# Feed-forward output projections by seven half-size products (Strassen) in a two-layer hybrid trunk

## The chip, the cores and the metric

The kernel runs on one core of one Trainium2 chip. The metric is device time in microseconds (us), median of several runs; lower is better. TensorE (PE) multiplies matrices, with its weight loads listed apart as PEld; VectorE (DVE), ScalarE (ACT) and GpSimd (POOL) do elementwise work; SyncE (SP) issues most DMAs. Each engine works through its own queue of instructions in order.

## What is computed

A decoder trunk of two layers on x, 512 tokens by 1024 features, in float32. Each layer has a token mixer (gated linear attention, GLA, in the first; gated DeltaNet, GDN, in the second) and then a gated convolutional feed-forward layer. After each of these four sublayers stands a layer norm of a scaled residual:

```python
D_MODEL, SEQ, D_FF, ALPHA = 1024, 512, 2816, 4 ** 0.25

def conv_ffn(x, w_in, conv_w, w_out):            # w_in 1024 x 5632, w_out 2816 x 1024
    h = causal_dwconv(x @ w_in, conv_w)          # 3 taps along the tokens, per channel
    gate, up = jnp.split(h, 2, axis=-1)
    return (jax.nn.gelu(gate, approximate=False) * up) @ w_out

for i in range(2):
    y = gla_mixer(h, ...) if i == 0 else gdn_mixer(h, ...)
    h = layer_norm(ALPHA * h + y, ln_g[i, 0], ln_b[i, 0])
    h = layer_norm(ALPHA * h + conv_ffn(h, ...), ln_g[i, 1], ln_b[i, 1])
```

## The kernel before, in words

The code numbers the sublayers 0 (GLA), 1 (feed-forward), 2 (GDN) and 3 (feed-forward); "layer 1" and "layer 3" below are the two feed-forward ones.

**Precision.** Every projection multiplies two float32 operands, each split into a rounded part and its residue (`split_out`, L450: ScalarE casts `wh`, VectorE subtracts for `wl`, both on L451). A product is three matmuls: high by high, high by low, low by high (`tm_terms`, L362; all matmuls are issued in `mm`, L161).

**Layout.** x lies transposed in SBUF as `xh` and `xl` (feature blocks by tokens). An up-projection item (`fm_items`, L339) makes one block of 128 hidden features by 512 tokens in a PSUM bank `fm`: 8 input blocks times 3 terms, 24 matmuls of 128x512. While the layer norm before it is not done, the first four items (`HEADSTART`) are done in two halves of 256 tokens, so that they can start with the first two token blocks. For each of the 22 feature blocks there is a gate item and an up item. `ffn` (L719) runs three taps on each (`ffn_conv`: ScalarE L714, VectorE L716 twice), a Gelu on the gate (L726), their product (L731), and splits the result into `gh` and `gl`.

**Output projection before.** The 22 feature blocks are taken in two chunks (`CHUNKS`: 12 and 10). After the items of a chunk, `out_proj` (L403) multiplies by the rows of w_out: for each half of the 1024 output columns, four PSUM banks `tm` (one per block of 128 tokens, `tb`) accumulate over the pairs of feature blocks (`tm_half`, L367). When a bank is done, VectorE adds it to the residual `h` (L412 the first time with ALPHA, then L414). In the last chunk it also takes statistics (L419) and starts the layer norm of that token block; there the last four pairs of the second half (`TAIL`) are done token block by token block, with their weights held in slots, so that the layer norms start one after another.

**Layer norm.** `ln_stats` (L588) aggregates the statistics; `ln` (L606) normalizes h, transposes it on TensorE (`xT`), applies gain and bias on ScalarE (`xf`) and writes `xh` and `xl`; after the last sublayer `ln_out` (L652) does the final norm on VectorE and stores.

**Weights.** `plan` lists the weight tiles in order of use. `issue` (L221) loads one of 128x1024 from HBM into `raw` (3 buffers, `RAWB`) on SP's queue and splits it into `wh` and `wl` (4 buffers each, `WB`); `prefetch` does so `LOOKAHEAD` (2) tiles ahead in the order of the program. That order is a priority: the queue of each engine is filled at build time, with what is ready first. `self.clk` and `self.dve` are the program's own estimates of TensorE's and VectorE's time; generators (`spawn`, `pump`) emit side work, such as layer norms, when that clock has reached their due time.

**Memory.** One SBUF pool of 53 slots of 128x512 (`slot`) serves all sublayers, the residual and the split activations too; constants have their own pool (`keep`). PSUM has 8 banks (`psum`).

Of the kernel before, what the change touches and what calls it, by code (L numbers as in the profile page):

```python
# [25 lines left out]
ALPHA = 4.0 ** 0.25  # L26
LN_EPS = 1e-5
# [3 lines left out]
CHUNKS = ((0, 12), (12, 22))  # L31
SLOTS = 53
# [16 lines left out]
def blk(i, n=P):  # L49
    return slice(i * n, i * n + n)  # L50


class Trunk:
# [3 lines left out]
    def __init__(self, ctx, tc):  # L57
        self.tc = tc
        self.nc = nc = tc.nc
        self.n = 0  # L60
        ec = ctx.enter_context
        ap = ec(tc.tile_pool(name="acts", bufs=1))
        self.xh = ap.tile([P, NC, S], F32R, name="xh", tag="xh")
        self.xl = ap.tile([P, NC, S], F32R, name="xl", tag="xl")
        self.wp = ec(tc.tile_pool(name="wts", bufs=WB))
        self.mp = ec(tc.tile_pool(name="mem", bufs=SLOTS))
# [4 lines left out]
        self.dp = ec(tc.tile_pool(name="scratch", bufs=1, space=bass.MemoryType.DRAM))  # L71
        self.ident = self.keep([P, P], "ident")
# [5 lines left out]
        self.reset = self.keep([P, S], "reset")  # L78
        nc.vector.memset(self.reset, 1.0)
        nc.vector.memset(c4(self.reset)[:, :, 0:1], 0.0)  # L80
        self.h = None
        self.plan = []
        self.issued = 0
        self.taken = 0
# [12 lines left out]
        self.late = []  # L97
        self.first = None
        self.between = None
# [5 lines left out]

    def slot(self, s, dt=F32):
        return self.mp.tile([P, S], dt, name=self.uid(s), tag="slot")
# [4 lines left out]
    def small(self, shape, s, dt=F32, bufs=None):  # L112
        return self.sp.tile(shape, dt, name=self.uid(s), tag=s, bufs=bufs)

# [41 lines left out]
    def mm(self, out, a, b, start=True, stop=True):  # L156
# [4 lines left out]
        t = self.nc.tensor.matmul(out, a, b, start=start, stop=stop)  # L161
# [54 lines left out]

    @staticmethod
    def in_slots(item):
        return item[0] == "tm" and item[5]

    def issue(self, item):  # L221

        nc = self.nc
        if item[0] == "rep":
            return self.issue_rep(*item[1:])
        raw = self.rp.tile([P, 1024], F32, name=self.uid("raw"), tag="raw")
# [57 lines left out]

    def prefetch(self):
        while self.issued < min(len(self.plan), self.taken + self.look):
            item = self.plan[self.issued]
            if self.held == WB and not self.in_slots(item):
                break
            self.ready.append(self.issue(item))  # L290
            self.issued += 1

# [46 lines left out]
    def fm_items(self, items):  # L339

        start = 0 if all(self.is_set(("x", tb)) for tb in range(NTB)) else HEADSTART
        first = items[:start]
        ws, banks = [], []
        for half in range(2 if first else 0):
            self.wait(("x", 2 * half), ("x", 2 * half + 1))
            for i, f in enumerate(first):
                if not half:
                    ws.append(self.weight())
                    banks.append(self.psum("fm"))
                self.fm_mms(banks[i], ws[i], half * 256, half * 256 + 256, self.pin and not half and i < 2)  # L350
                if half:
# [10 lines left out]
    def tm_terms(self, ps, ah, al, wh, wl, first, last):  # L362
        self.mm(ps, ah, wh, first, False)
        self.mm(ps, ah, wl, False, False)
        self.mm(ps, al, wh, False, last)
# [137 lines left out]
    def load_x(self, x):  # L503

        nc = self.nc
        self.h = [[self.slot("h") for _ in range(2)] for _ in range(NTB)]
# [99 lines left out]
    def ln(self, tb, spill=False):  # L606
# [36 lines left out]
        yield from self.until(("x", NTB - 1))  # L643
# [8 lines left out]
    def ln_out(self, tb, out):  # L652
        nc = self.nc
        gb, h = self.ln_gb(), self.h[tb]

        def center(mv):
            for hf in range(2):
                nc.vector.scalar_tensor_tensor(h[hf], h[hf], mv[:, 0:1], gb[hf], ALU.subtract, ALU.mult)

        mv, rs = self.ln_stats(tb, center)  # L660
        for hf in range(2):
            m = 2 if tb == NTB - 1 and hf else 1
            for i in range(m):
                cols = blk(i, S // m)
                nc.vector.scalar_tensor_tensor(h[hf][:, cols], h[hf][:, cols], rs, gb[2 + hf][:, cols],
                                               ALU.mult, ALU.add)
                (nc.sync, nc.scalar)[i].dma_start(out[blk(tb), hf * S + cols.start:hf * S + cols.stop],
                                                  h[hf][:, cols])
        yield 0.0

    def unspill(self, gb_rows):
# [4 lines left out]
        for hf in range(2):  # L676
            for tb in range(NTB):
                t = self.slot("h")
# [17 lines left out]
    def ffn_plan(self, w_in, w_out):  # L696
        for f0, f1 in CHUNKS:
# [3 lines left out]
            self.plan_out(w_out, f0 * P, f1 - f0, TAIL if f1 == NF else 0)  # L701
# [8 lines left out]
    def ffn_conv(self, ps, cw, b):  # L710
        nc = self.nc
        a = self.slot("conv")
# [6 lines left out]
    def ffn(self, cw, li, g, b, final, out=False):  # L719
        nc = self.nc  # L720
        for ci, (f0, f1) in enumerate(CHUNKS):
            gs, act, items = [], {}, []
            for f in range(f0, f1):
                def gate(ps, f=f):
                    a = self.ffn_conv(ps, cw, f)
# [3 lines left out]
                def up(ps, f=f):  # L729
                    u = self.ffn_conv(ps, cw, NF + f)  # L730
                    nc.vector.tensor_mul(u, u, act.pop(f))  # L731
                    t = self.slot("gh", F32R), self.slot("gl", F32R)
                    self.split_out(*t, u)
                    gs.append(t)
# [3 lines left out]
            last = ci == len(CHUNKS) - 1  # L738
# [5 lines left out]
            a = lambda c, tb: (gs[c][0][:, blk(tb)], gs[c][1][:, blk(tb)])  # L744
            self.out_proj(a, f1 - f0, ci == 0, final if last else None, 2 if last and out else 1)
# [38 lines left out]
    def gla_consts(self, w_gk2, b_gk, norm_w):  # L784
        nc = self.nc

        self.gk2 = self.keep([96, S], "gk2", F32R)
# [13 lines left out]
        self.gla_nw = self.keep([P, 256], "gla_nw")  # L801
# [8 lines left out]
        self.gla_mask = self.keep([P, S], "gla_mask", U8)  # L810
        nc.gpsimd.tensor_copy(self.gla_mask, mk)
        self.b_gk = self.keep([P, 4], "gla_b")
        self.spawn(self.columns([(b_gk.rearrange("(n p) -> n p", p=P), 4, self.b_gk)]), 12.0)

    def gla(self, li, g, b):
# [83 lines left out]
        ss = self.keep([P, GH, 4], "gla_ss")  # L899
        rr = self.keep([P, GH, 4], "gla_rr")  # L900
# [89 lines left out]
    def mixer_out(self, y, li, g, b, final=None):  # L990
# [7 lines left out]
        self.out_proj(a, NC, True, self.ln)  # L998

# [24 lines left out]
    def gdn_conv(self, ps, b):  # L1024

        nc = self.nc
        a = self.slot("conv")
# [8 lines left out]
    def gdn(self, li, g, b):  # L1036
        nc = self.nc
        self.flags = {f: t for f, t in self.flags.items() if f[0] in ("x", "h")}
        hs = slice(H0, H0 + 8)
        al = self.gdn_al  # L1040
        spilled = self.gb_rows
        keep = lambda s: self.keep([P, DH, 4], s)
        eb, neb, ebl, cd = (keep(s) for s in ("gd_eb", "gd_neb", "gd_ebl", "gd_cd"))
        bn, bp, rk = keep("gd_bn"), keep("gd_bp"), keep("gd_rk")
        ssq, rr = self.keep([P, 2, DH, 4], "gd_ssq"), self.keep([P, DH, 4], "gd_rr")
        bt = self.keep([P, 4, 64], "gd_bt")
# [7 lines left out]
        def ba_done(ps):  # L1054
# [8 lines left out]
            ea = self.keep([P, 1], "gd_ea")  # L1063
# [50 lines left out]
        def k_done(ps, hd):  # L1114
            k[hd] = self.gdn_conv(ps, 8 + hd)
# [4 lines left out]
        def q_done(ps, hd):  # L1120
            q[hd] = self.gdn_conv(ps, hd)
# [134 lines left out]
        def v_done(ps, hd):  # L1256
            vc[hd % 2] = self.gdn_conv(ps, 16 + hd)
# [145 lines left out]
def kernel(  # L1403
# [41 lines left out]
    t.drain()  # L1445

# [28 lines left out]
```

## Time and profile before

| | |
|---|---|
| median of 3 runs | 1276.69 us (1276.61 to 1277.08) |
| profiled execution: first to last instruction | 1274.8 us (the page gives no other time for it; the median lies 1.9 above) |
| matmuls | 6682 |
| busy: PE, VectorE, ScalarE, GpSimd | 1260.9, 785.5, 552.2, 112.5 us |
| DMA | 126.53 MB, mean 99 GB/s |
| mean granted TensorE clock | 0.999 |

How to read it: the page is one execution. "Busy" counts the instructions of an engine; matmuls overlap in the array, so the sum of their durations is more than the time that they take. A row of a group or of the timeline gives start, duration, engine, line, operation, output and inputs, shape, and in brackets the idle time before it and who ended that. A row of waits gives who waited for whom, total us, times, longest. A row of the chain gives start, us, and what. A row of a stretch gives its bounds and length, then busy time (and number) of PE, PEld, VectorE, ScalarE, GpSimd, then granted clock, DMA share and GB/s.

### The profile page before, as it was taken

How to read it: one execution, taken by the hardware profiler on the slowest of the kernel's cores; microseconds unless marked ns; L12 is line 12 of the kernel's file. 1: busy time of each engine (PE TensorE's matmuls, PEld its weight loads, DVE VectorE, ACT ScalarE, POOL GpSimd, SP SyncE). 2: the span in 40 equal slices, each digit the busy share in tenths (PEclk: the TensorE clock that was granted, in tenths of full speed). 3: DMA queues.
4: the chain of work that ended last, by engine and by line, in shares of the span. 5: the costliest groups of instructions: out<-in, count | busy, mean ns of one | idle time of the engine just before them, and what ended most of it. 6: DMA issues, size and time to landing. Idle time of an engine off the chain costs nothing.

```text
span 1274.8 us, 17225 instructions
## 1 busy us (share of the span) xinstructions
PE 1260.9 (99%) x6682; PEld 1068.4 (84%) x6682; DVE 785.5 (62%) x1383; ACT 552.2 (43%) x1042; POOL 112.5 (9%) x152
## 2 busy tenths in 40 slices
PE   8999999999999999999999999999999999999997
PEld 8878888988888888889888888988988888888886
DVE  4953556676643466555789955679587653366656
ACT  4644444544421244435765544543644431244430
POOL 4000000070000000001023120100053000000000
PEclk9999999999999999999999999999999999999999
DMA  7322224143333333351354431234053333333331
GB/s 207 112 70 63 67 93 123 50 132 99 99 99 99 99 92 92 98 151 66 103 149 113 122 75 51 68 116 137 17 152 101 94 96 99 99 99 99 94 105 66
DMA packets 167234, 126.53 MB, mean 99 GB/s; under 512 B 16104, under 2 KB 139818, under 8 KB 167152
## 3 DMA queue, kind: packets, MB, share of 16 engines
q1 hardware_dynamic: 162064, 116.28, 31.1%
q0 software_dynamic: 3888, 8.50, 2.3%
q8 instruction: 52, 0.85, 0.3%
q10 hardware_dynamic: 1200, 0.66, 0.2%
q14 instruction: 30, 0.25, 0.1%
HBM read 119.63 MB, written 5.78 MB: 98 GB/s over the span
## 4 chain that ended last, share of the span: by engine, by line
PE 94%; DVE 3%; ACT 1%; DMA 1%; issue 1%; SPq 0%; DVEq 0%; ACTq 0%
PE fm L161 50%; PE tm L161 35%; PE o L161 2%; PE xT L178 1%; PE R L161 1%; PE V L161 1%; DVE wl L451 1%; PE qkT L178 1%; PE vn L161 1%; PE pq L161 1%; PE pg L161 1%; PE yT L178 1%; PE s L161 0%; DMA h<-in_x_dram 0%; PE qs L161 0%
## 5 line engine op out<-in xcount | busy, mean ns | idle before, releaser
L451 DVE TENSOR_TENSOR wl<-raw,wh 128x1024 fp32r<-128x1024 f32 (+1 forms) x190 | 237.8, 1253 | 312.2 <-ACT wh L451 312.0
L161 PE MATMUL fm<-xh,wh 128*128 128x512 f32 (+2 forms) x1104 | 402.6, 367 | 0.7 <-ACT xh L451 0.7
L161 PE MATMUL fm<-xl,wh 128*128 128x512 f32 (+2 forms) x1104 | 399.9, 365 | 0.0
L161 PE MATMUL fm<-xh,wl 128*128 128x512 f32 (+1 forms) x1088 | 396.0, 366 | 0.0
L451 ACT CAST wh<-raw 128x1024 fp32r<-128x1024 f32 (+1 forms) x190 | 199.0, 1047 | 279.4 <-PE tm L161 166.8
L161 PEld LDWEIGHTS fm<-xh,wh 128*128 128x128 f32 (+1 forms) x1104 | 206.9, 188 | 33.7 <-ACT xh L451 0.9
L161 PEld LDWEIGHTS fm<-xl,wh 128*128 128x128 f32 (+1 forms) x1104 | 207.0, 188 | 32.4
L161 PEld LDWEIGHTS fm<-xh,wl 128*128 128x128 f32 x1088 | 204.2, 189 | 33.5
L716 DVE SCALAR_TENSOR_TENSOR conv<-fm,ffn_cw,conv 128x511 f32<-128x511 f32 (+1 forms) x176 | 130.8, 746 | 3.0
L161 PE MATMUL tm<-wl,gh 128*128 128x512 f32 x290 | 112.4, 388 | 0.0
L161 PE MATMUL tm<-wh,gl 128*128 128x512 f32 x290 | 112.4, 388 | 0.0
L161 PE MATMUL tm<-wh,gh 128*128 128x512 f32 x290 | 112.4, 388 | 0.0
L451 ACT CAST gh<-conv 128x512 fp32r<-128x512 f32 x44 | 27.3, 621 | 124.2 <-DVE conv L731 124.1
L161 PE MATMUL tm<-wh,xh 128*128 128x512 f32 x192 | 78.5, 409 | 0.8 <-ACT qk L836 0.8
L161 PE MATMUL tm<-wh,xl 128*128 128x512 f32 x192 | 75.2, 392 | 0.0
L161 PE MATMUL tm<-wl,xh 128*128 128x512 f32 x192 | 75.0, 390 | 0.0
L726 ACT ACTIVATE conv<-conv 128x512 f32<-128x512 f32 x44 | 27.8, 632 | 94.8 <-DVE conv L716 94.8
L161 PEld LDWEIGHTS tm<-wh,gl 128*128 128x128 f32 x290 | 54.4, 188 | 11.2
L161 PEld LDWEIGHTS tm<-wl,gh 128*128 128x128 f32 x290 | 54.4, 188 | 11.2
L161 PEld LDWEIGHTS tm<-wh,gh 128*128 128x128 f32 x290 | 54.4, 188 | 11.1
L714 ACT ACTIVATE conv<-fm,ffn_cw 128x512 f32<-128x512 f32 x88 | 60.0, 682 | 0.2
L647 POOL TENSOR_TENSOR h<-h,gb 128x512 f32<-128x512 f32 x16 | 27.1, 1716 | 344.3 <-DMA gb<-in_ln_g_dram 235.8
(280 smaller groups left out, 1556.5 us busy)
## 6 DMA issues: line engine op xcount, KB each, us to landing
raw<-in_ffn_w_in_dram SPq DMA_DIRECT2D x88, 512.0 KB, 3.8
raw<-in_ffn_w_out_dram SPq DMA_DIRECT2D x44, 512.0 KB, 3.8
raw<-in_gdn_w_in_dram SPq DMA_DIRECT2D x32, 512.0 KB, 4.0
raw<-in_gla_w_in_dram SPq DMA_DIRECT2D x23, 512.0 KB, 3.6
raw<-in_gla_w_out_dram SPq DMA_DIRECT2D x8, 512.0 KB, 3.7
raw<-in_gdn_w_out_dram SPq DMA_DIRECT2D x8, 512.0 KB, 3.8
h<-in_x_dram SPq DMA_DIRECT2D x8, 256.0 KB, 4.3
hd<-h POOLq DMA_DIRECT2D x8, 256.0 KB, 2.5
```

Of the source, the lines that this page charges most:

```text
L161: t = self.nc.tensor.matmul(out, a, b, start=start, stop=stop)
L178: t = self.nc.tensor.transpose(out, a, self.ident[:n, :n])
L451: return self.nc.scalar.copy(dst_h, src), self.nc.vector.tensor_sub(dst_l, src, dst_h)
L647: nc.gpsimd.tensor_mul(h[hf], h[hf], gb[hf])
L714: nc.scalar.activation(a, ps, AF.Identity, scale=tap(2))
L716: nc.vector.scalar_tensor_tensor(a[:, d:], ps[:, :S - d], tap(2 - d), a[:, d:], ALU.mult, ALU.add)
L726: nc.scalar.activation(a, a, AF.Gelu)
```

## The change

The output projections of both feed-forward layers are computed by Strassen's scheme (Winograd's form, seven products). Tokens are halved (blocks 0, 1 and 2, 3), output columns are halved, and the hidden features are halved into even and odd blocks. A pair of blocks gives the activation quarters a11, a22, a12 and the sums w1, v2, v3, v4: four VectorE operations of 128x256 per pair in place of none, and one split of 1792 columns instead of two of 512. The weight quarters are b11, b12, b22, b21; t1 to t4 are running sums of them, made in place by VectorE. The products come in the order b11, b21, t1, t2, b22, t3, t4 and accumulate in three pairs of PSUM banks; after each product VectorE adds or subtracts the two banks to or from a half row of `h` (`update`). Blocks are taken in three groups (8, 8, 6) instead of two chunks. Token blocks 2 and 3 are complete after b22, blocks 0 and 1 after t4; `halves` therefore turns the order of the first four items of the next sublayer round. In the last group each norm starts when its block is complete; `TAIL` is no longer used here. During the products the weights are taken 3 ahead, and loads 2 further (`AHEAD`).

The slot pool is opened anew for each sublayer (`stage`), with 45 slots for the mixers and 6 for the feed-forward layers beside the new tiles; the residual has its own pool of 8 (`resid`), which also holds GDN's keys. Some constants move into the stage pools (`own`), and `reset` is written again in layer 2.

```diff
-CHUNKS = ((0, 12), (12, 22))
-SLOTS = 53
+FORMS = ("a11", "a22", "a12", "w1", "v2", "v3", "v4")
+FOLD_ALL = {"b11": ("a11", 0), "t1": ("w1", 2), "t2": ("v2", 0), "b21": ("a12", 1), "t3": ("v3", 0), "b22": ("v4", 2),
+            "t4": ("a22", 0)}
+FOLD_NEW = {"b11": "b11", "t1": "b12", "t2": "b22", "b21": "b21", "t3": None, "b22": None, "t4": "b21"}
+GROUPS = ((0, 8), (8, 16), (16, 22))
+SLOTS = 45
+FFN_SLOTS = 6
+FOLDED = 6
+AHEAD = 2
...
+    def stage(self, name, slots):
+        if self.mp is not None:
+            self.mp.release()
+        self.mp = self.tc.alloc_tile_pool(name=name, bufs=slots, reuse_waits="tile")
...
+    def fold_load(self, group, quarter, i):
...
+        if quarter == "b21":
+            t = self.rp.tile([P, 1024], F32, name=self.uid("raw"), tag="raw")
+        else:
+            t = self.mp.tile([P, 1024], F32, name=self.uid(quarter), tag="folded", bufs=FOLDED)
...
+    def issue_fold(self, group, name, quarter, i):
...
+        t = get({"b21": "b21", "t3": "b12", "b22": "b22"}.get(name, "b11"))
+        other = {"t1": "b12", "t2": "b22", "t3": "b22", "t4": "b21"}.get(name)
+        if other:
+            nc.vector.tensor_add(t[:, cols], t[:, cols], get(other)[:, cols])
...
+        self.split_out(wh[:, cols], wl[:, cols], t[:, cols])
...
     def prefetch(self):
         while self.issued < min(len(self.plan), self.taken + self.look):
+            self.load_ahead(self.issued + 1)
...
+        self.load_ahead(self.taken + self.look + AHEAD)
...
-        for half in range(2 if first else 0):
+        for turn, half in enumerate(self.halves if first else ()):
...
+                def up(ps, f=f, f1=f1):
+                    odd = (f - f0) % 2
...
+                    if f + 1 == f1:
+                        split(256, 768)
+                    part = lambda i: t[:, blk(i, 256)]
+                    nc.vector.tensor_sub(part(4), part(0), part(2))
+                    nc.vector.tensor_sub(part(5), part(4), part(1))
+                    nc.vector.tensor_sub(part(6), part(1), part(0))
+                    nc.vector.tensor_add(part(7), part(5), part(3))
+                    if f + 1 == f1:
+                        split(768, 1792)
+                    else:
+                        split(0, 1792)
...
-            self.out_proj(a, f1 - f0, ci == 0, final if last else None, 2 if last and out else 1)
+            self.folded(forms, gi == 0, final if last else None)
+
+    def folded(self, forms, first, final):
...
+        def update(name, r, ps):
...
+            if at in fresh:
...
+                nc.vector.scalar_tensor_tensor(h, h, ALPHA, ps, ALU.mult, op)
+            else:
+                nc.vector.tensor_tensor(h, h, ps, op)
...
+            if last and done[at] == (1 if at == low else 2):
+                nc.vector.bn_stats(st[tb][:, hf, :], h)
...
+                    self.spawn(final(tb))
...
+        self.look = 3
+        for name, _, form, at in FOLD:
+            f = FORMS.index(form) * 256
+            for i in range(0, m, 2):
+                w = self.weight()
+                n = min(2, m - i)
+                for r in range(2):
+                    ps = banks[at][r]
+                    for j in range(n):
+                        _, fh, fl = forms[i + j]
+                        cols = slice(f + r * P, f + r * P + P)
...
+                        self.tm_terms(ps, fh[:, cols], fl[:, cols], *w[j], begin, end, True)
+                    if i + 2 >= m:
+                        update(name, r, ps)
+                    self.pump()
+                self.spend()
+        self.look = LOOKAHEAD
+        if last:
+            self.halves = (1, 0)
```

More of the change, by code (lines that the diff above doesn't have):

```diff
@@ L113, in small, with own @@
         return self.sp.tile(shape, dt, name=self.uid(s), tag=s, bufs=bufs)
+    def own(self, shape, s, dt=F32):
+        return self.mp.tile(shape, dt, name=self.uid(s), tag=s, bufs=1)
     def keep(self, shape, s, dt=F32):
@@ L160, in mm @@
         self.clk += n * (0.00045 if b.dtype == F32R else 0.00175)
-        t = self.nc.tensor.matmul(out, a, b, start=start, stop=stop)
+        t = self.nc.tensor.matmul(out, a, b, start=start, stop=stop, skip_group_check=joined)
         if self.pin:
@@ L215, in plan_out, with plan_fold @@
                 self.plan_tm(w, row + 2 * cp * P, min(2, n - 2 * cp), hf * S, hf == 1 and cp >= npair - tail)
+    def plan_fold(self, w, f0, f1):
+        group = {"w": w, "f0": f0, "m": (f1 - f0) // 2}
+        for name, quarter, _, _ in FOLD:
+            for i in range(0, group["m"], 2):
+                self.plan.append(("fold", group, name, quarter, i))
     @staticmethod
@@ L291, in prefetch, with load_ahead @@
             self.issued += 1
+        self.load_ahead(self.taken + self.look + AHEAD)
+    def load_ahead(self, until):
+        self.loaded = max(self.loaded, self.issued)
+        while self.loaded < min(len(self.plan), until) and self.plan[self.loaded][0] == "fold":
+            _, group, _, quarter, i = self.plan[self.loaded]
+            if quarter:
+                self.fold_load(group, quarter, i)
+            self.loaded += 1
     def weight(self):
@@ L642, in ln @@
             return
-        yield from self.until(("x", NTB - 1))
+        for i in range(NTB):
+            yield from self.until(("x", i))
         yield RESID_DELAY + 10.0 * tb
@@ L743, in ffn @@
                     self.ln_gb()
-            a = lambda c, tb: (gs[c][0][:, blk(tb)], gs[c][1][:, blk(tb)])
-            self.out_proj(a, f1 - f0, ci == 0, final if last else None, 2 if last and out else 1)
+            self.folded(forms, gi == 0, final if last else None)
+    def folded(self, forms, first, final):
+        nc = self.nc
+        m = len(forms)
+        last = final is not None
+        if last:
+            self.sqrt_table()
+        banks = [[self.psum("fold") for _ in range(2)] for _ in range(3)]
+        uses = [[n for n, _, _, at in FOLD if at == i] for i in range(3)]
+        fresh = {(tb, hf) for tb in range(NTB) for hf in range(2)} if first else set()
+        st = {tb: self.small([P, 2, 6], "ln_st") for tb in range(NTB)} if last else None
+        done = {}
+        def update(name, r, ps):
+            low, high = (r, 0), (r, 1)
+            top, right = (2 + r, 0), (2 + r, 1)
+            at, op = {"b11": (top, ALU.add), "t1": (high, ALU.add), "t2": (right, ALU.subtract), "b21": (top, ALU.add),
+                      "t3": (high, ALU.subtract), "b22": (right, ALU.add), "t4": (low, ALU.add)}[name]
+            tb, hf = at
+            h = self.h[tb][hf]
+            if at in fresh:
+                fresh.remove(at)
+                self.wait(("h", tb, hf))
+                nc.vector.scalar_tensor_tensor(h, h, ALPHA, ps, ALU.mult, op)
+            else:
+                nc.vector.tensor_tensor(h, h, ps, op)
+            self.vec(0.7, self.clk + 0.4)
+            done[at] = done.get(at, 0) + 1
+            if last and done[at] == (1 if at == low else 2):
+                nc.vector.bn_stats(st[tb][:, hf, :], h)
+                self.vec(0.7)
+                if all(done.get((tb, i), 0) == (1 if (tb, i) == low else 2) for i in range(2)):
+                    self.st = st
+                    self.spawn(final(tb))
[5 more added lines that the diff above has]
+                w = self.weight()
+                n = min(2, m - i)
+                for r in range(2):
[3 more added lines that the diff above has]
+                        cols = slice(f + r * P, f + r * P + P)
+                        begin = name == uses[at][0] and i + j == 0
+                        end = i + j == m - 1
+                        self.tm_terms(ps, fh[:, cols], fl[:, cols], *w[j], begin, end, True)
+                    if i + 2 >= m:
+                        update(name, r, ps)
+                    self.pump()
+                self.spend()
+        self.look = LOOKAHEAD
+        if last:
+            self.halves = (1, 0)
```

124 lines of the change are left out of this document (81 added, 43 removed).

## The prediction

> **What bounds the kernel now.** I read the page's list of engines first, then who waited for whom on TensorE, then the chain that ended last, in order of time.
>
> ```profile
> PE 1260.9 (99%) x6682; PEld 1068.4 (84%) x6682; DVE 785.5 (62%) x1383; ACT 552.2 (43%) x1042; POOL 112.5 (9%) x152
> PE warm L523 <- DVE reset L80: 1.7, 1, 1.7
> 359.33 65.28 PE tm L161 x288
> 424.61 108.80 PE fm L161 x480
> 1211.83 54.82 PE tm L161 x270
> ```
>
> TensorE (PE) is busy 99% of the span and its longest wait is 1.7 us. Inside a feed-forward layer the chain is TensorE alone: no other engine appears between the 288 output-projection matmuls and the 480 up-projection matmuls. Matmuls are pipelined, so their listed duration is not their price; the chain gives it: 65.28/288 and 108.80/480 are both 0.2267 us per 128x512 matmul. Removing a matmul there saves 0.2267 us as long as TensorE stays the bound. The question is whether it does, so the next views are VectorE (DVE) and ScalarE (ACT): busy time by stage, then single instructions.
>
> ```profile
> 1040.00:1100.00 60.00, 60.00 (x267) 49.67 (x266) 18.78 (x20) 12.22 (x12) 0.00 (x0) 1.00 0.33 97
> 556.46 1.23 DVE L451 TENSOR_TENSOR wl<-raw,wh 128x1024 fp32r<-128x1024 f32 x1 [1.03 <-ACT wh L451]
> 557.60 1.28 DVE L414 TENSOR_TENSOR h<-h,tm 128x512 f32<-128x512 f32 x2
> 558.80 1.28 DVE L419 BATCH_NORM_STATS2 ln_st<-h 128x6 f32<-128x512 f32 x2
> 559.99 1.34 DVE L414 TENSOR_TENSOR h<-h,tm 128x512 f32<-128x512 f32 x2
> 560.65 1.06 ACT L451 CAST wh<-raw 128x1024 fp32r<-128x1024 f32 x1 [4.22 <-PE tm L161]
> 459.30 1.53 DVE L716 SCALAR_TENSOR_TENSOR conv<-fm,ffn_cw,conv 128x511 f32<-128x511 f32 x2
> 460.86 0.69 DVE L731 TENSOR_TENSOR conv<-conv,conv 128x512 f32<-128x512 f32 x1
> 1264.09 0.40 DVE L414 TENSOR_TENSOR h<-h,tm 128x256 f32<-128x256 f32 x1
> 458.02 0.68 ACT L714 ACTIVATE conv<-fm,ffn_cw 128x512 f32<-128x512 f32 x1
> ```
>
> In the first row, 60 us inside an output projection, the 60.00 is TensorE's busy time and the 18.78 VectorE's: there is room. Starts give the price of one instruction in a full queue: a 1024-wide two-operand one 1.14 us (556.46 to 557.60), a 512-wide one 0.60 (two in 1.20), a statistic 0.60 (558.80 to 559.99). A 256-wide one takes 0.40 in a dependent chain.
>
> **The change, part by part.** *Removed.* A layer's output projection is 22 feature blocks x 4 token blocks x 2 halves x 3 terms = 528 matmuls. Seven products of 11 pairs x 2 row blocks x 3 terms are 462, of the same shape. 66 fewer per layer, 132 in all: 132 x 0.2267 = **29.9 us** gained.
>
> *Added on VectorE.* Take a group of 8 feature blocks (4 pairs; two per layer). TensorE now needs 7 x 4 x 6 x 0.2267 = 38.1 us. It uses 14 weight tiles, each of them 12 matmuls or 2.7 us. VectorE does 14 residues of the splits (14 x 1.14 = 16.0), 8 sums of weight quarters (8 x 1.14 = 9.1; t1 to t4, two tiles each; the row of the residue stands for it, both have two operands in SBUF) and 14 updates of the residual (14 x 0.60 = 8.4): 33.5. At its start stands the last pair's work, which 5 pairs of cover hid before: taps 1.53, product 0.69, residue 0.60, four sums 1.6, residue 1.14 = 5.6, after a ScalarE pass of 0.7. Three tiles can be split ahead, as many are owed to the next group, so 39.8 against 38.1. Sums of t1 and t3 need only loaded quarters and may run earlier, in the up-projections, where VectorE has time: up to 4 x 1.14 = 4.6 less. So the group is short by between -2.9 and 1.7 us; when both engines are this full, one pass through sum, cast and residue (1.14 + 1.06 + 1.14 = 3.3) can show as well. Bounds 0 to 5, taken 2 (near the balance): four groups, **8 us** lost.
>
> *The last group of layer 1* has 3 pairs: 28.6 us of TensorE (7 x 18 x 0.2267). Its tiles are one full and one half tile per product. VectorE: splits 7 x 1.74 = 12.2, sums 4 x 1.74 = 7.0, updates 8.4, last pair 5.6, and then the layer norm.
>
> ```profile
> 571.53 0.69 DVE L414 TENSOR_TENSOR h<-h,tm 128x512 f32<-128x512 f32 x1 [3.13 <-PE tm L161]
> 572.98 0.21 DVE L592 BATCH_NORM_AGGREGATE ln_mv<-ln_st 128x2 f32<-128x12 f32 x1
> 574.28 0.54 DVE L616 TENSOR_SCALAR h<-h,ln_mv,ln_rs 128x512 f32<-128x512 f32 x1
> 577.59 0.43 DVE L629 CAST xh<-xf 128x512 fp32r<-128x512 f32 x1 [2.77 <-ACT xf L625]
> 577.93 0.68 DVE L414 TENSOR_TENSOR h<-h,tm 128x512 f32<-128x512 f32 x1
> 579.73 0.68 DVE L633 TENSOR_TENSOR xl<-xf,xh 128x512 fp32r<-128x512 f32 x1
> 590.53 6.47 PE fm L161 x54
> ```
>
> Eight statistics are 4.8. A token block's norm costs VectorE 1.84 (572.98 to 574.82), a cast of 0.34 and two residues of 0.60: 3.4. The next stage begins with token blocks 2 and 3, so two norms (6.8) stand before it: 12.2 + 7.0 + 8.4 + 5.6 + 4.8 + 6.8 = 44.8, less 2.9 split ahead, plus 1.1 for the next weight, plus 0.7: 43.7 against 28.6, so TensorE waits 15.1. If t1's and t3's sums run early, 3.5 less; if t4's two updates and their statistics come after those norms, 2.4 less. Bounds 9.2 to 15.1, taken 12.5. The norms of blocks 0 and 1 have as cover four items' first halves, 96 matmuls at 6.47/54 = 0.12 us = 11.5; one block takes 8.8 (from its update at 571.53 to 580.3), a second one 3.4 more: 12.2, so 0.5 to 1 shows. Together **13 us**. Today the layer norms hide under four pairs kept back for each token block.
>
> *The last group of layer 3* ends the program.
>
> ```profile
> 1251.49 0.21 DVE L592 BATCH_NORM_AGGREGATE ln_mv<-ln_st 128x2 f32<-128x12 f32 x1
> 1253.77 1.42 DVE L665 SCALAR_TENSOR_TENSOR h<-h,ln_rs,gb 128x512 f32<-128x512 f32 x2
> 1266.65 0.02 issue
> 1271.04 0.40 DVE h L665
> ```
>
> The final norm costs 3.7 us per block (1251.49 to 1255.19). All VectorE work from the last up-projection matmul on: 12.2 + 7.0 + 8.4 + 5.6 + 4.8 + 4 x 3.7 - 2.9 + 0.7 = 50.6 us, or 47.1 with 3.5 of sums done early. After its last instruction (1271.44) 3.4 us pass to the end of the span. That makes 50.5 to 54.0, against 28.6 of matmuls and today's 8.15 from the last matmul (1266.65) to 1274.8: 36.8. Loss 13.7 to 17.2, taken **15.5 us**.
>
> *The clock.* A long wait may cost beyond its length:
>
> ```profile
> 1266.70:1270.70 4.00, 0.00 (x0) 0.00 (x0) 3.79 (x11) 0.30 (x1) 0.00 (x0) 1.00 0.34 128
> 1272.20:1273.00 0.80, 0.00 (x0) 0.00 (x0) 0.00 (x0) 0.00 (x0) 0.00 (x0) 0.50 0.99 327
> ```
>
> After the last matmul at 1266.65 the granted clock (third figure from the right) was still 1.00 to 1270.70 and 0.50 from 1272.20: at least 4 us of idleness halve it. My wait before layer 2 is cut up by the layer norm's transposes and by t3 and t4, so I take 0; the bound above is the four first halves at half speed, 11.5 us. The Trainium skill (TensorE: Matmul & The Clock Gate, section "What's actually happening") says that an idle window of about 3.4 us halves the clock and a busy one of 3.4 us restores it; the rows agree on the fall, none shows the rise, and by that page one such wait would be an estimated 1.7 us and the forecast 1285.0.
>
> *With one answer.* Pools by stage: a tile waits for the old tile at its place, but the feed-forward layer's first write follows a whole item (24 x 0.2267 = 5.4 us) after the mixer's last reads; 0 taken, 5.4 if a place is held. The two memsets of the reset row in layer 2 add about 1 us to a VectorE that is late already: inside the bounds. Output weights are loaded 55 tiles' worth instead of 44, b21 twice:
>
> ```profile
> raw<-in_ffn_w_out_dram SPq DMA_DIRECT2D x44, 512.0 KB, 3.8
> ```
>
> A load lands in 3.8 us, is issued two tiles (5.4 us) or more ahead, and DMA was 0.33 busy in the stage's row: 0, or 3.8 once per group if a load waits on SP's queue for a quarter's buffer, with the loads queued behind it. Casts add ScalarE work of 1.06 per 2.7 us tile: hidden.
>
> **The sum.** -29.9 + 8 + 13 + 15.5 = +6.6 us. The profiled execution's span is 1274.8, so 1281.4; the runs' median of 1276.69 is 1.9 above that span, hence **1283.3 us**, slower by 0.5%. The comparison can tell about 0.2% (2.6 us) from no change.
>
> **The rivals.** *A: the forecast*, VectorE becomes the bound of the last group and a near-equal of TensorE in the others. 0.55, 1276 to 1307: the upper end has 5 us in each of four groups, 16.1 and 17.2 in the last two, one 3.3 chain and a third of the clock's 11.5, a loss of 60.4 (1276.7 + 30.5).
>
> *B: the products pay* (faster). If VectorE does t1's and t3's sums during the up-projections, the four groups lose nothing, and the last two 9.2 and 13.7: 22.9, so 1276.7 - 29.9 + 22.9 = 1269.7. The point from which it decides is 29.9 us of losses in all. For it: the order on an engine is already mixed by readiness (in the last timeline rows above an update stands between a cast and a residue of a norm), and VectorE is 62% busy. Against: what is late is one stage's work, and that stage's excess of 15 us has no cover. 0.27, 1264 to 1274.
>
> *C: the waits in a row.* If sum, cast and residue of a tile stand one after the other in VectorE's queue, it is idle during each cast.
>
> ```profile
> DVE wl L451 <- ACT wh L451: 312.0, 144, 6.2
> ```
>
> That wait is VectorE's longest today, harmless as TensorE is the bound. A tile then costs 3.3 + 0.3 of handing over, a t product of two tiles 7.3 + 1.2 of updates = 8.5 instead of 5.4: 3.1 x 16 = 49 in the four groups instead of 8, and about 10 more in the last ones: 1283.3 + 51 = 1334. Against: the weight tiles are handed on three ahead, and quarters are there early. 0.10.
>
> *D: it doesn't do what it says*: the matmuls go but banks or buffers hold the next group's up-projections back by as much, and nothing is left: 1274 to 1279. t3 and t4 share a bank, so t4's first matmul must await t3's update; 6 of 8 banks are held. 0.08.
>
> **How the numbers follow.** The forecast is A's 1283.3. The range of 1266 to 1307 leaves out C and a piece of B's lower end. Faster by over 0.2%: B, 0.27. Within 0.2%: D, 0.08 (A's lower edge and B's upper one cancel). Slower: A and C, 0.65. A's own range is 1276 to 1307.
>
> **What would show it.** TensorE: 924 matmuls into the fold banks at 0.2267 us where nothing waits; its waits before them name VectorE (residue or update), few in the groups of four pairs, 12 us or more around t3, t4 and the first items of layer 2. VectorE: busy over 85% inside each projection, above 95% in the last ones, and 950 us or so in all. The last matmul would lie 15 us or more before the span's end rather than 8, or wait during t3 and t4. I am wrong if sums sit in the up-projection stage and the projections of 3 pairs run near 29 us (B), or if VectorE shows long waits for casts within the projections (C), or if waits name PE banks or DMA (D).

## The result and the profile after

The changed kernel takes 1277.72 us (median of 12 runs, 1276.51 to 1278.71) against 1276.93 us for the kernel before (12 runs): ratio 1.0007, 95% interval 0.9999 to 1.0015. No difference can be measured. The forecast was 1283.3 us and a slower kernel; the range of 1266 to 1307 holds the time. The profiled execution's span is 1275.5 us, 0.7 above that of before.

The page after: engines, then the two groups that the change brought, with count, busy us, mean ns of one, idle before it and releaser.

```profile
PE 1244.2 (98%) x6520; PEld 1044.7 (82%) x6520; DVE 951.9 (75%) x1593; ACT 594.7 (47%) x1064; POOL 117.2 (9%) x152
L188 PE MATMUL fold<-wh,fh 128*128 128x512 f32 x308 | 122.5, 401 | 8.3 <-DVE ln_t L684 6.4
L534 DVE TENSOR_TENSOR wl<-b,wh 128x1024 fp32r<-128x1024 f32 x72 | 80.2, 1129 | 4.6 <-ACT wh L534 4.4
```

The first group is one of the three terms: 3 x 308 = 924 matmuls, as the scheme says. VectorE works 951.9 us. The waits of TensorE (us in total, times, longest) and the chain around layer 1's projections (start, us):

```profile
PE fold L188 <- DVE ln_t L684: 6.4, 1, 6.4
PE xT L205 <- DVE h L699: 6.3, 2, 5.7
PE fold L188 <- ACT wh L534: 0.4, 2, 0.2
```

```profile
185.88 30.40 PE tm L188 x132
...
232.32 84.03 PE fm L188 x444
316.35 33.59 PE fold L188 x144
...
350.40 5.64 PE fold L188 x24
...
547.22 2.81 PE fold L188 x12
...
842.62 19.25 PE tm L188 x84
...
910.06 84.03 PE fm L188 x444
...
1224.94 2.81 PE fold L188 x12
```

Two readings. In a group of four pairs the chain is TensorE alone, but 33.59/144 is 0.2333 us per matmul and not 0.2267. In the last groups the chain leaves TensorE after 12 matmuls (547.22, 1224.94) and is mostly VectorE's from there; TensorE's two long waits lie there and at the norm behind layer 1's.

Stretches of after: first group of layer 1, its last group, then layer 3's last group and the wait in it. Columns: PE, PEld, VectorE, ScalarE, GpSimd busy (number), granted clock, DMA share, GB/s.

```profile
316.35:355.60 39.25, 39.25 (x169) 31.50 (x169) 34.49 (x41) 17.21 (x18) 0.00 (x0) 1.00 0.52 158
547.20:581.30 34.10, 31.82 (x141) 24.61 (x140) 33.46 (x58) 16.18 (x22) 3.27 (x6) 1.00 0.27 71
1224.90:1250.80 25.90, 25.68 (x109) 19.74 (x107) 25.24 (x37) 11.25 (x14) 0.00 (x0) 1.00 0.00 1
1250.80:1257.20 6.40, 0.08 (x1) 0.00 (x0) 6.40 (x19) 1.21 (x3) 0.00 (x0) 0.79 0.09 31
```

VectorE is 88% busy in the group of four pairs (34.49 of 39.25) and 97 to 100% in the last groups. To place the loss, points of the chain of before stand against the same points of after (232.32, 842.62 and 910.06 above):

```profile
185.81 29.97 PE tm L161 x132
...
231.80 127.53 PE fm L161 x636
...
842.30 19.08 PE tm L161 x84
...
910.21 127.53 PE fm L161 x636
```

| Part, in the profiled executions | worked out | us |
|---|---|---|
| 132 matmuls fewer | 132 x 0.2267 | -29.9 |
| four groups of 4 pairs | (33.59 + 5.64 - 168 x 0.2267) x 4 | +4.6 |
| the two mixers' output projections | GLA: 232.32 - 231.80 = 0.5; GDN: (910.06 - 842.62) - (910.21 - 842.30) = -0.5 | 0.0 |
| layer 1's last group, with the start of layer 2 | (842.62 - 232.32) - (842.30 - 231.80) = -0.2; + 14.95 - 2.3 | +12.5 |
| layer 3's last group | (1275.5 - 910.06) - (1274.8 - 910.21) = +0.85; + 14.95 - 2.3 | +13.5 |
| sum | | +0.7 |

The 14.95 is half of the 29.9, the 2.3 half of the 4.6. The three losses are smaller than forecast. The mixers' code is the same, and still their matmuls are slower (132 of them take 30.40 us, 29.97 before); in GDN that is made up for, because a wait of 1.0 us for a layer norm (`PE xT L178 <- DVE ln_mv L592`) is there before and not after. Neither this nor the 0.2333 was forecast, and nothing in the waits explains the slower pace.

### The profile page after: what moved, and what is told of

The parts are those of the page before. It is cut to its first block, busy times and chain, and to the rows that moved or that the text cites. A ratio compares the mean times of both kernels' runs of the same rounds, so it can differ in the third digit from the quotient of the medians.

```text
span 1275.5 us, 17191 instructions
## 1 busy us (share of the span) xinstructions
PE 1244.2 (98%) x6520; PEld 1044.7 (82%) x6520; DVE 951.9 (75%) x1593; ACT 594.7 (47%) x1064; POOL 117.2 (9%) x152
## 4 chain that ended last, share of the span: by engine, by line
PE 90%; DVE 7%; ACT 2%; issue 1%; DMA 0%; SPq 0%; DVEq 0%; ACTq 0%
PE fm L188 50%; PE tm L188 17%; PE fold L188 13%; DVE wl L534 2%; PE o L188 2%; PE xT L205 1%; DVE h L877 1%; PE R L188 1%; PE V L188 1%; PE qkT L205 1%; PE vn L188 1%; PE pq L188 1%; PE pg L188 1%; PE yT L205 1%; DVE ln_st L881 0%
## 5 line engine op out<-in xcount | busy, mean ns | idle before, releaser
L188 PE MATMUL fold<-wh,fh 128*128 128x512 f32 x308 | 122.5, 401 | 8.3 <-DVE ln_t L684 6.4
L188 PE MATMUL fold<-wl,fh 128*128 128x512 f32 x308 | 122.6, 398 | 0.0
L188 PE MATMUL fold<-wh,fl 128*128 128x512 f32 x308 | 122.5, 398 | 0.0
L534 ACT CAST wh<-b 128x1024 fp32r<-128x1024 f32 x72 | 69.2, 980 | 96.4 <-PE fold L188 40.0
L534 DVE TENSOR_TENSOR wl<-b,wh 128x1024 fp32r<-128x1024 f32 x72 | 80.2, 1129 | 4.6 <-ACT wh L534 4.4
L188 PEld LDWEIGHTS fold<-wh,fh 128*128 128x128 f32 x308 | 58.1, 190 | 24.9 <-issue 6.8
L188 PEld LDWEIGHTS fold<-wl,fh 128*128 128x128 f32 x308 | 58.4, 189 | 14.2 <-DVE wl L534 0.5
L188 PEld LDWEIGHTS fold<-wh,fl 128*128 128x128 f32 x308 | 58.3, 189 | 14.1
L799 DVE SCALAR_TENSOR_TENSOR form<-fm,ffn_cw,form 128x511 f32<-128x511 f32 x88 | 65.6, 745 | 1.8 <-ACT form L797 0.4
L799 DVE SCALAR_TENSOR_TENSOR conv<-fm,ffn_cw,conv 128x511 f32<-128x511 f32 x88 | 65.5, 744 | 1.1
```

Source lines behind the costliest of these rows:

```text
L188: t = self.nc.tensor.matmul(out, a, b, start=start, stop=stop, skip_group_check=joined)
L534: return self.nc.scalar.copy(dst_h, src), self.nc.vector.tensor_sub(dst_l, src, dst_h)
L799: nc.vector.scalar_tensor_tensor(a[:, d:], ps[:, :S - d], tap(2 - d), a[:, d:], ALU.mult, ALU.add)
```

## Experiments

**Pace by the place of the operands.** TensorE is never late in the groups of four pairs and still a matmul takes 0.0067 us longer. What differs between the kernels there, beside the data, is where the two operands lie in SBUF. One operand of a matmul is loaded ahead, 128x128 at a time, in the PEld rows (the stationary one: in a feed-forward output projection `fh` and `fl`, before `gh` and `gl`, in a stage pool or slots); the other is the 128x512 operand of the PE rows (the moving one: `wh` and `wl`). Byte addresses in a partition, from the two compiled programs:

```
                               before     after
weights wh, wl (first buffer)   49280     49280
slots / stage pools begin at    82048    116640
distance, modulo 256                0        32
```

The first theory is that the pace follows this distance; its rival is that a TensorE beside a VectorE that is 88% busy is slower. Two kernels, one for each kernel of the comparison: 224 more bytes of constants after the change, 32 bytes between weights and slots before it.

`aligned`:

```diff
+        nc.gpsimd.memset(self.keep([P, 56], "pad"), 0.0)
```

> The changed kernel with 224 bytes of padding per partition in the constants' pool, so that the stage pools begin at a multiple of 128 bytes again (116864) instead of at 32 past one (116640). Theory 1 (place in SBUF: a matmul whose stationary tile lies 32 bytes off a 128-byte line, while the moving tile lies on one, takes 0.2333 us rather than 0.2267): the fold matmuls fall to 0.2267, a projection of 4 pairs from 39.2 to 38.1 us, the mixers' last projections from 30.40 to 29.97; with the last groups bound by VectorE 5 to 7 us in all, so 1271 to 1273. Theory 2 (the fold matmuls are slowed by VectorE's traffic in SBUF while it is full): nothing changes, 1277.7.

`before_shift`:

```diff
         self.wp = ec(tc.tile_pool(name="wts", bufs=WB))
+        nc.gpsimd.memset(ec(tc.tile_pool(name="shift", bufs=1)).tile([P, 8], F32, name="shift", tag="shift"), 0.0)
         self.mp = ec(tc.tile_pool(name="mem", bufs=SLOTS))
```

> The kernel before with its slot pool moved by 32 bytes, nothing else. Theory 1: the output-projection matmuls with weights from the weight pool (moving wh, wl) and activations from slots (stationary gh, gl, yh, yl) go from 0.2267 to 0.2333 us, about 1050 of them, so 7 us slower: 1284. The tail's (moving wsh, wsl, in slots like the stationary ones) stay at 0.2267. Theory 2: 1277, all at 0.2267.

Measured: `aligned` 1272.30 us, ratio to the kernel before 0.9967 (0.9954 to 0.998); `before_shift` 1284.10 us, ratio 1.0054 (1.0038 to 1.007). The chains, of `aligned` first:

```profile
185.71 29.95 PE tm L189 x132
...
315.68 32.93 PE fold L189 x144
...
441.25 32.64 PE fold L189 x144
...
474.34 5.65 PE fold L189 x24
```

```profile
186.32 30.40 PE tm L162 x132
...
360.32 67.19 PE tm L162 x288
427.52 108.81 PE fm L162 x480
```

In the second group 32.64/144 is 0.2267 again, with VectorE as busy as it was. In the first, 32.93, the pace is the same but for one break of 0.3 us, in which a residue of VectorE's ends late. And the kernel before, with its computation untouched, slows to 67.19/288 = 0.2333 in the output projections alone. So the slower pace comes from the memory layout and not from VectorE. It also explains the mixers: 30.40 in `before_shift` and 29.95 in `aligned`. In the shifted kernel the weights that are held in slots, beside activations in slots, keep their pace (36 of them in layer 1's tail take 8.18 us in both kernels) while those in `wh` need 0.2333.

Three more layouts of the kernel before ask whether it is the distance between the operands or the absolute place, and after how many bytes places count as the same again (that length is called the line below). `shift_both` puts the 32 bytes ahead of the weights (so that weights and slots move together, against `xh`); `shift_64` and `shift_256` are `before_shift` with 64 and 256 bytes.

> The kernel before with the weight pool and the slot pool both moved by 32 bytes; xh and xl stay. If what counts is whether stationary and moving tile lie alike, the output-projection matmuls (wh with gh, both 32 off) stay at 0.2267 us and the up-projections (stationary wh 32 off, moving xh not) go to 0.2333: some 2600 matmuls, 17 us slower, 1294. If only a stationary tile that is off counts, both go to 0.2333: 1301. If only the moving tile counts, the output projections alone: 1284.

> The kernel before with its slot pool moved by 64 bytes: if a line of 64 bytes is what counts, all matmuls stay at 0.2267 us and the time at 1277; if one of 128 bytes, the output projections go to about 0.2333 and the time to 1284.

> The kernel before with its slots moved by 256 bytes against the weight pool; nothing else changes. If the line within which the two operands have to stand alike is 256 bytes long, the time is that of the kernel before, 1277 us, and output-projection matmuls keep 227 ns. If it is 512 bytes or longer, 1284 us and 233 ns, as with 32 and 64 bytes.

Measured, one run each: 1293.80, 1284.01 and 1277.04 us. The chains of the three in this order:

```profile
364.42 65.29 PE tm L162 x288
429.71 112.00 PE fm L162 x480
```

```profile
360.26 67.20 PE tm L162 x288
427.46 108.83 PE fm L162 x480
```

```profile
359.64 65.28 PE tm L162 x288
424.93 108.80 PE fm L162 x480
```

When weights and slots move together, the output projections are back at 0.2267 (65.29/288) and the up-projections, whose `xh` stayed, go to 0.2333 (112.00/480): the distance counts. At 64 bytes the pace is slow, at 256 it is whole, and in `hybrid` below, at 128 bytes, it is slow too. So the line is 256 bytes, as far as these distances tell. What in the chip does this was not found.

**Is VectorE the bound of the groups?** `no_sums` leaves out the sums of the weight quarters for t1 to t4 (48 VectorE instructions; that part of the computation is missing). If VectorE sets the time of a group, the group gets shorter.

```diff
-        if other:
+        if other == "never":
```

> The changed kernel without the sums of weight quarters (t1 to t4 take the quarter alone; this leaves out part of the computation). If VectorE's work binds the last group of a layer, its 7.0 us of sums per layer, less what is done ahead in the up-projections (about half), come off each: 7 to 12 us in all, 1266 to 1271, and the projections of 4 pairs stay at 39.2 us, as VectorE keeps up there. Rival: the last groups are bound by the order of the queues (norms in front of t3's updates, casts waited for) rather than by the sum of the work: under 3 us, 1275 or more.

Measured: 1267.58 us, ratio 0.9923 (0.9909 to 0.9937). Its chain:

```profile
316.49 33.59 PE fold L188 x144
...
906.07 84.03 PE fm L188 x444
...
1220.85 20.31 PE fold L188 x87
```

The first group still takes 33.59 us for 144 matmuls: VectorE does not bind there. All the gain is in the last groups, 4.0 us in layer 1 (906.07 against 910.06; the mixers hold no such sums) and 5.2 in layer 3 (906.07 to the end at 1266.3 is 360.2, against 365.4). The last groups are bound by VectorE, as forecast.

**The order in VectorE's queue.** After's timeline of the end shows one placement that costs TensorE its 6.4 us:

```profile
1251.42 1.40 DVE L742 SCALAR_TENSOR_TENSOR h<-h,ln_mv,gb 128x512 f32<-128x512 f32 x2
...
1256.46 0.67 DVE L877 TENSOR_TENSOR h<-h,fold 128x512 f32<-128x512 f32 x1
...
1262.89 1.39 DVE L877 TENSOR_TENSOR h<-h,fold 128x512 f32<-128x512 f32 x2 [2.44 <-PE fold L188]
```

The final norms of blocks 2 and 3 begin at 1251.42 and stand ahead of t3's update (L877, 1256.46), which frees the bank that t4 needs. `norm_late` starts those norms only behind t4's first update:

```diff
-                    self.spawn(final(tb))
-                    self.pump()
+                    (late if tb >= 2 else now).append(tb)
...
+                        if name == "t4" and r == 0:
+                            now = late + now
+                        while now:
+                            self.spawn(final(now.pop(0)))
```

> The changed kernel with the layer norms of token blocks 2 and 3 emitted behind t4's first update instead of after b22. If the order of VectorE's queue costs (the norms of 2 and 3 stand before t3's updates, which t4's matmuls need), the wait of 6.4 us before t4 in layer 3 goes, t4 runs at full clock, and VectorE no longer idles 2.4 us there: 2 to 4 us in layer 3; in layer 2's start the norms of 2 and 3 come later by what t4 gains: -1 to +3. Together 1273 to 1278. Rival, the work alone binds: 1277.7 less at most VectorE's idle 2.4.

Measured: 1276.33 us, ratio 0.9994 (0.9985 to 1.0003). The longest wait of a fold matmul that is left, and the start of layer 3's full-width items in the chain:

```profile
PE fold L188 <- ACT wh L534: 2.9, 4, 1.2
```

```profile
912.46 84.03 PE fm L188 x444
```

The 6.4 us wait is gone and layer 3 is 2.5 us shorter (1275.4 - 912.46 = 362.9 against 365.4). But that start is 2.4 us later (912.46 against 910.06): in layer 1 the same order delays the norms with which layer 2 begins (their first transposes start at 583.94 instead of 576.80). VectorE has the same work; the order only chooses who waits.

**The sums on another engine.** `sums_pool` gives the sums to GpSimd, which was 9% busy.

```diff
-            nc.vector.tensor_add(t[:, cols], t[:, cols], get(other)[:, cols])
-            self.vec(0.62 * n)
+            nc.gpsimd.tensor_add(t[:, cols], t[:, cols], get(other)[:, cols])
```

> The changed kernel with the sums of weight quarters on GpSimd instead of VectorE. If VectorE's work binds the last groups, this takes as much off as leaving the sums out did (9 us), if GpSimd's longer time per sum (1.7 us per 512 columns in the residual's rows, so 3.4 for a full tile) stays hidden by the loads and tiles ahead: 1268 to 1272. Rival: three sums of one quarter follow each other (t1, t2, t4), each with a split between, and GpSimd's 3.4 us lengthens that chain, or it slows VectorE: 1277 or more.

Measured: 1300.76 us, ratio 1.0184 (1.0167 to 1.0201): the rival's case. Its timeline inside the first group, and its longest wait on TensorE:

```profile
332.46 3.26 POOL L347 TENSOR_TENSOR b<-b,b 128x1024 f32<-128x1024 f32 x1 [3.36 <-DVE wl L533]
333.45 3.36 DVE L533 TENSOR_TENSOR fl<-form,fh 128x1024 fp32r<-128x1024 f32 x1
335.69 3.36 POOL L347 TENSOR_TENSOR b<-b,raw 128x1024 f32<-128x1024 f32 x1
336.73 1.27 DVE L876 TENSOR_TENSOR h<-h,fold 128x512 f32<-128x512 f32 x2
```

```profile
PE fold L188 <- DVE fl L533: 14.2, 8, 3.2
```

A sum takes 3.3 us instead of 1.2, and a VectorE residue beside it 3.36 instead of 1.22: it ends at 336.81, after GpSimd's first sum (335.72). Two updates at 336.73, beside the second sum, take their usual 1.27; they read one operand from PSUM. The Trainium skill (SBUF — State Buffer, section "SBUF: two separate sides") says that GpSimd and a VectorE instruction with two SBUF inputs share one pair of ports that is held for the whole instruction, so that the other blocks; these rows agree. The sums did not leave VectorE's time, they took more of it: VectorE is busy for 965.1 us, after the change 951.9 with the sums on it.

**Products only where VectorE keeps up.** The loss is in the last groups, so `hybrid` uses the seven products in the first two groups of each layer and plain products (eight, without sums) in the third, with three pairs held back for the norms as before the change. 96 matmuls are removed instead of 132, and the plain weights of the tail lie in the stage pool. It started from `aligned`.

```diff
-            self.plan_fold(w_out, f0, f1)
+            if f1 == NF:
+                self.plan_out(w_out, f0 * P, f1 - f0, PLAIN)
+            else:
+                self.plan_fold(w_out, f0, f1)
...
-            self.folded(forms, gi == 0, final if last else None)
+            if last:
+                a = lambda c, tb: (gs[c][0][:, blk(tb)], gs[c][1][:, blk(tb)])
+                self.out_proj(a, f1 - f0, False, final, 2 if out else 1)
+            else:
+                self.folded(forms, gi == 0, None)
```

> The seven products in the two groups of 8 feature blocks only; the last group of 6 by the plain output projection of before (tail of three pairs, token block by token block, with its layer norms), and the stage pools at a multiple of 128 bytes. If the loss sits in the last groups alone, 4 groups x 24 matmuls fewer x 0.2267 = 21.8 us are kept: 1277.0 - 21.8 = 1255, up to 1257 with the few tenths that a projection of 4 pairs still loses. Rival: the loss goes with the end of a layer (fewer matmuls left there to cover the norms: 72 a half instead of 120): 1260 or more, with waits of TensorE at the start of layer 2.

Measured: 1265.59 us, ratio 0.9911 (0.9896 to 0.9926), 9 to 11 us above what was expected and where the rival put it (1260 or more). Its constants had moved the stage pools to 116992, 128 bytes off the weights' line, and the fold ran at 0.2324 us (33.47 for 144). `hybrid2` is the same kernel with a pad of 24 instead of 56 columns, which puts the pools at 116864:

> The kernel with Strassen products in the first two groups of each layer and plain products in the last (the experiment `hybrid`), with its stage pools moved by another 128 bytes less, so that the fold's stationary and moving tiles stand at the same place within 256 bytes again (in `hybrid` they stood 128 bytes apart). Theory 'the pace of a matmul follows the relative place of its two operands, within a line of 256 bytes or more': fold matmuls at 227 ns instead of 233, four groups x 1.2 us and two mixers x 0.45 us less, so 1265.6 - 5.7 = 1259.9 us (1259 to 1261). Rival 'the line is 128 bytes and what slowed `hybrid` is the busier VectorE': no change, 1265 to 1266.

Measured: 1261.11 us (1259.26 to 1262.47), ratio 0.988 (0.9863 to 0.9898); the profiled execution, at 1259.26, has a span of 1257.6. Its chain:

```profile
441.15 32.64 PE fold L191 x144
...
1214.42 20.41 PE tm L191 x90
...
1253.78 0.40 DVE h L756
```

The fold is back at 0.2267, and this is the fastest version of the study, 1.2% faster than the kernel before; its median lies just above the 1259 to 1261 that was expected. It would have to give 96 x 0.2267 = 21.8 us; the spans give 17.2 (the profiled execution was the fastest of four; the medians give 15.9). The rest goes at the end of both layers, as the rival of `hybrid` had it. At the start of layer 2 TensorE waits for the norm:

```profile
PE fm L191 <- DVE xh L719: 1.7, 1, 1.7
```

In layer 3, behind these 90 matmuls (1234.83), the chain is VectorE's alone to 1254.18, norm after norm: that layer gains 8.3 us (356.3 from the start of its full-width items against 364.6) instead of 10.9. Six blocks leave a token block 18 matmuls (4.1 us) of cover, and the first block takes VectorE 5.2 us there. With other group sizes this could shrink; that was not tried.

## Why the prediction was wrong

It forecast slower by 6.6 us; in the profiled executions the change costs 0.7. By its own steps:

*132 matmuls, 29.9 us.* Right in number; right in price where the operands lie alike (`aligned`, 32.64/144). As built, each of 924 matmuls cost 0.0067 us more, 6.2 us in all, part of it hidden in the last groups.

*Four groups of four pairs, 8 us.* This is the step that failed. The prediction set 39.8 us of VectorE against 38.1 of TensorE and took 2 us a group "near the balance". In truth VectorE kept up and the group lost 1.15 us, nearly all of it pace: `aligned` takes 0.7 to 1.0 of it off with VectorE unchanged, and `no_sums`, with less VectorE work, takes off nothing. In `aligned` the first group of a layer takes 32.93 + 5.61 us and the second 32.64 + 5.65, against 38.1: 1.3 us in all four is the most that VectorE can have cost there, and as built even that is hidden. That the 4.6 of the table stands near the 8 is luck, as it has another cause. The prediction's lower bound of 0 was nearly right: three of the eight sums run ahead in the up-projections, as these rows of after show (the folds begin at 316.35).

```profile
303.88 1.22 DVE L347 TENSOR_TENSOR b<-b,b 128x1024 f32<-128x1024 f32 x1
307.62 1.21 DVE L347 TENSOR_TENSOR b<-b,b 128x1024 f32<-128x1024 f32 x1
311.86 1.21 DVE L347 TENSOR_TENSOR b<-b,b 128x1024 f32<-128x1024 f32 x1
```

3 x 1.14 = 3.4 us less makes 36.4 against 38.1. With work ready ahead, the near-equal engine cost next to nothing; the 3.3 us chain of sum, cast and residue showed as no more than the 0.3 us break in `aligned`.

*Layer 1's last group, 13 us.* Right in mechanism (TensorE waits 5.7 us for the norm's L699, the longest of the two on the page), 12.5 measured, inside 9.2 to 15.1 plus what shows of blocks 0 and 1.

*Layer 3's last group, 15.5 us.* Right in mechanism (6.4 us for L684), 13.5 measured, just under the bound of 13.7. From 1224.94 to the end pass 50.6 us; the sum of VectorE's work had given 50.5 to 54.0. The last matmul ends 12 us before the end instead of 8, with the wait in t4 as named.

*The clock, 0.* Wrong. It fell in both waits. Stretches of after, from the wait before layer 2 into its first items:

```profile
582.00:584.00 2.00, 0.00 (x0) 0.00 (x0) 2.00 (x4) 2.00 (x7) 0.71 (x2) 1.00 0.90 234
584.00:586.00 2.00, 0.00 (x0) 0.00 (x0) 1.86 (x10) 2.00 (x8) 0.00 (x0) 0.88 0.40 43
586.00:588.00 2.00, 0.58 (x3) 0.59 (x4) 2.00 (x8) 2.00 (x6) 0.34 (x1) 0.50 0.90 239
590.00:592.00 2.00, 2.00 (x12) 2.00 (x11) 0.94 (x2) 2.00 (x7) 0.39 (x1) 0.50 0.87 324
592.00:594.00 2.00, 2.00 (x17) 2.00 (x17) 0.87 (x2) 2.00 (x7) 0.00 (x0) 0.92 0.02 8
```

The transposes did not cut the wait up: from 581.4 to 587.4 TensorE did next to nothing. The clock (third figure from the right) fell after some 4 us and rose again about 5 us after work began (587.41). In layer 3 the 15 fold matmuls behind the wait took 5.59 us instead of 3.5: 2.1 us, in layer 1 about as much (16 transposes 3.68 us, against 0.87 for 8 at full clock: 1.9). Both are inside the 12.5 and 13.5, so what VectorE itself cost there was less than forecast. The Trainium skill (TensorE: Matmul & The Clock Gate, section "What's actually happening") gives windows of about 3.4 us for both, which run freely; the rows above fit that. The 1.7 us that the prediction estimated from that page for one such wait was nearer than the 0.

*Pools by stage, 0.* Wrong for a reason that was not thought of: no write waits for an old tile, but the pools' new place slowed every matmul that takes `wh` against them. That makes up nearly all of the 4.6 us in the groups, and 0.5 us or so in each mixer; `aligned` gives 5.4 us back at the median (1277.72 - 1272.30).

The difference of 5.9 us is thus -3.4 (groups), -0.5 and -2.0 (last groups), 0.0 (mixers). That it is no larger is partly luck. VectorE was to cost 8 + 13 + 15.5 = 36.5 us; without the clock's 4 us the last groups lost about 22, and in the other four VectorE cost nothing that shows. The layout and the clock, which the sum had at 0, filled over half of that gap. The signs that the prediction named for A came true, VectorE's 951.9 us and its 88% in the groups among them; they could not tell A from B, because an engine can be that busy without being late.

Of the rivals, B's condition (the groups lose nothing, the last two 9.2 and 13.7) comes close to `aligned`, whose 1272.30 lies in B's 1264 to 1274; as built, the layout takes that gain back and leaves what D named, nothing, without D's cause. C is refuted: VectorE waited 4.4 us in all for casts of the weight tiles that take part in sums (the group of 72 residues above), where C had 3.1 us for each of 16 products, and TensorE's fold matmuls waited 0.4 us for casts.

## What to carry to other kernels

Where an instruction count is cut on the busiest engine, look at the stage in which another engine takes over the work and has no later stage to do it in: here the four inner groups kept the gain of their eighth of the matmuls (all but 1.3 of 21.8 us where the layout was right), and the two before a norm lost 26 us for 8.2 gained, so the scheme belongs in the inner groups only. A near-equal engine with work ready ahead cost next to nothing inside a stage and all that it was behind at its end. After any change of buffers, read the start-to-start pace of one matmul group in the chain before and after: a layout that shifts one operand by less than a line cost more here than all the added VectorE work did in the four groups.

## What the runs showed of the hardware

- Here a 128x512 matmul from split float32 took 0.2267 us where its stationary and moving tiles began at the same place modulo 256 bytes of SBUF (distances 0 and 256), and 3% more at distances of 32 and 64 (0.2333 us) and 128 bytes (0.2324). No wait shows it.
- A VectorE instruction with two SBUF operands, 1.22 us alone, took 3.36 beside a GpSimd sum (`sums_pool`); one with an operand in PSUM kept its time (two in 1.27 us).
- In layer 1 the granted clock halved about 4 us into TensorE's wait and came back about 5 us after work resumed; in layer 3 both took about 4 us (0.79 on average in the wait's row, and 0.83 in the us from 1261.00, with work from 1257.27).
